# Two-layer hybrid decoder trunk: the RWKV blocks of the mixing projection move to 5th, 10th and 15th place, and a pair's preparation is placed after the tail two pairs back

## The chip, the cores and the metric

One core of one Trainium2 chip runs the whole program. The metric is the device time of one execution in microseconds (us). Runs of the kernel before are compared by their median; a profile is one further execution, recorded by the hardware profiler.

## The reference

The kernel computes two decoder layers over 256 tokens of width 2048, in float32. Each layer is a token-mixing part and a feed-forward part, each between two RMS norms:

```python
for l in range(DEPTH):                                   # DEPTH = 2
    u = rms_norm(h, norm_pre_mix[l])
    p = u @ w_in[l]
    p_ret, p_hgrn, p_ml, p_rw = split_cols(p, GROUP_COLS)
    o_ret  = retention_group(p_ret)
    o_hgrn = hgrn2_group(p_hgrn, ...)
    o_ml   = mlstm_group(p_ml, ...)
    o_rw, v_first = rwkv7_group(p_rw, v_first, ...)
    mixed = concatenate([o_ret, o_hgrn, o_ml, o_rw]) @ w_out[l]
    h = h + rms_norm(mixed, norm_post_mix[l])
    u = rms_norm(h, norm_pre_ffn[l])
    h = h + rms_norm((silu(u @ w_ffn_gate[l]) * (u @ w_ffn_up[l])) @ w_ffn_down[l], norm_post_ffn[l])
```

Each of the four groups has 8 heads of 64. The change concerns the RWKV-7 group, a recurrence over time with a full state matrix per head:

```python
state = state * exp(lw_t) - (state @ kk_t) (a_t * kk_t)^T + v_t k_t^T
y_t   = state @ r_t
```

## The kernel before

A matmul of float32 is made from three: each weight is split in a high and a low part, and so is the activation; hi·hi, hi·lo and lo·hi are summed. SyncE (SP) loads the weights in units (L239), ScalarE (ACT) makes `w_hi` (L247) and VectorE (DVE) `w_lo` (L248), TensorE (PE) multiplies (L300 is the helper of all matmuls, L304 of all transposes). GpSimd (POOL) does little.

The projection of the mixing stage is cut into 31 blocks of 256 columns. A block is 96 matmuls of 256 columns, called *main* matmuls here, and fills one of three accumulator banks in PSUM, `acc_85`, `acc_86` and `acc_87` (the name ends in a buffer number). The first three blocks are `lora`, `rwv0` and `rwv1`. The others follow the list `SEQ` (L78): an entry ("rw", j) is one block with the receptance and key columns of RWKV pair j (two heads), and an entry of another group (ml, hg, rt) is four blocks for half of that group's heads. So the RWKV blocks stand at places 4, 9, 14 and 19 of 31. The out projection follows with 288 wide matmuls of 512 columns and two narrow blocks.

Between the main matmuls stands the work on the heads, in many small steps that use all engines. A planner, `interleave`, writes the program: it counts TensorE's time in `self.pe` by an estimate, runs `stream` (the main matmuls) and, whenever the estimate says that a step of another process is due, places that step. `stream` is blocked when no bank is free, and then steps of the other processes follow each other with no main matmul between them. The engines then run their instructions in the order written, each waiting for semaphores. `settle` and `empty` drain a full bank: block rw_j goes with a token shift into `rk[j % 2]`, and not before pair j - 2 has read that buffer for the last time, which sets `rk_free`.

The work on RWKV pair j has three steps:

- `rw_head` (L1332), the preparation: decay, scan (`cpd`), the norm of the key over the head by matmuls `pr<-parts,blkr`, two reciprocals, and the operand `BK`. `head_proc` (L881) starts it after block rw_j is drained and `rw_mid` says that pair j - 1 is past its inner inverse.
- `rwkv` (L1379), the chain: the gram product `pr<-KVR,BK` into `G`; a 16-row triangular inverse on DVE (`sprod`, 15 steps), with its operands sent through DRAM on both sides (`LD`, L1410, and `XD`, L1449); the mask product `TDD`; then products that build the whole inverse, `pr<-TDD,LoT`, `pr<-TDD,rk` and `pr<-rk,TDD`, `pr<-kap,G` and `pr<-TT,kap`; then four sequential steps over the state `S`; then the output `pr<-S,KVR`. After `TT` is written (L1478), `rk` may be overwritten.
- `rw_tail` (L1531): layer norm over the head, the transpose `pr<-ident,kap`, the gate product `pr<-SG,gup`, and the result in `mx`. When both pairs of a half are done, `settle` splits `mx` into `m` for the out projection.

The buffers `rk`, `kap`, `ra` (a), `cpd`, `rwc` and `bonus` exist twice and are used by pair number modulo 2. Small products go to two further banks, `pr_88` and `pr_89`, in turn; `po_90` to `po_92` serve the other groups, and at the end of the stage the out projection too.

Of the kernel before, what the change touches and what calls it, by code (L numbers as in the profile page):

```python
# [34 lines left out]
NEVER = 1e9  # L35
# [39 lines left out]

BLOCK_COLS = _block_cols()
GATE = {"ml": "mlo", "hg": "hgg", "rt": "rtg"}
SEQ = [("rw", 0), ("hg", 0), ("rw", 1), ("ml", 0), ("rw", 2), ("hg", 1), ("rw", 3), ("rt", 0), ("ml", 1), ("rt", 1)]  # L78
BLOCKS = ["lora", "rwv0", "rwv1"]
for _m, _i in SEQ:  # L80
    BLOCKS += [f"rw{_i}"] if _m == "rw" else [f"{_m}v{_i}", f"{_m}{2 * _i}", f"{_m}{2 * _i + 1}", f"{GATE[_m]}{_i}"]
# [190 lines left out]
class Trunk:  # L272
# [451 lines left out]
    def interleave(self):  # L724


        self.t0 = self.pe
        self.order = [x for x in SEQ if x[0] != "rw"]
        self.free = list(self.S)
        self.full, self.got, self.gate_at, self.head_at, self.rw_mid, self.rk_free = [], {}, {}, {}, 0, 0  # L730
        self.grp_fin, self.v_fin, self.proj_fin = 0, self.l == 0, False
        self.left = {key: 2 for key in MIXED}
        self.mh, self.ml = [None] * 8, [None] * 8
        self.yws = []
        self.procs = [[self.pe, self.rw_proc()], [self.pe, self.grp_proc()]]
        stream = self.stream()
        while stream is not None or self.procs:
            self.settle()
            now = [p for p in self.procs if self.ready(p) <= self.pe]
            if now:  # L740
                p = now[0]
                r = next(p[1], "end")
                if r == "end":
                    self.procs.remove(p)
                else:
                    p[0] = r if callable(r) else self.pe + r
                continue
            r = next(stream, "end") if stream is not None else "blocked"
            if r == "end":
                stream = None  # L750
            elif r == "blocked" and not self.settle():
                t = min([self.ready(p) for p in self.procs])
                assert t < NEVER
                self.pe = max(self.pe, t)
# [126 lines left out]
    def head_proc(self):  # L881
        for j in range(4):
            yield self.after(f"rw{j}", LAT)
            yield lambda: self.pe if self.rw_mid >= j else NEVER
            yield from self.rw_head(j)
            self.head_at[j] = self.pe + HEAD

# [643 lines left out]
    def rw_tail(self, j, out):  # L1531

        nc = self.nc
        c4, r, k, kap, a, cpd, rc, t2 = self.rw_parts(j)
        yt, yc = kap.rearrange("p (t h e) -> p h t e", t=2, h=2), self.F[3]
        mean, var = rc[:, 0:4], rc[:, 4:8]
        nc.vector.tensor_reduce(out=mean.rearrange("p (h t) -> p h t", h=2), in_=yt, axis=mybir.AxisListType.X, op=ALU.add)
        self.ts(mean, mean, -1.0 / HD)
        hts = [(2 * hh + t, hh, t) for hh in range(2) for t in range(2)]
        for g, hh, t in hts:  # L1540
            self.act(yc[:, 64 * g:64 * g + 64], yt[:, hh, t, :], AF.Square, bias=mean[:, g:g + 1], accum_out=var[:, g:g + 1])
        self.ts(var, var, 1.0 / HD, LN_EPS)
        self.pw(rc[:, 8:12], var, -0.5)
        for g, hh, t in hts:
            self.ts(yt[:, hh, t, :], yt[:, hh, t, :], mean[:, g:g + 1], rc[:, 8 + g:9 + g], ALU.add, ALU.mult)
        yield 4.5 + RLAT
        ps = self.ret_bank()
        for t in range(2):
            self.tr(ps[:, 128 * t:128 * t + 128], kap[:, 128 * t:128 * t + 128])
        self.stt(yc, ps[:, 0:256], self.pcol("ln_w", j), t2)  # L1550
        ps = self.ret_bank()
        self.mm(ps[:, 0:256], self.gup[:, 128 * j:128 * j + 128], self.SG)
        self.mul(out, yc, ps[:, 0:256])
        self.left["rw", j // 2] -= 1

    def run(self):
        self.setup()
        self.plan()
        self.l = 0
        self.first_norm()  # L1560
        for l in range(self.layers):
            self.mixing()
            self.ffn()
# [19 lines left out]
```

## Time and profile before

| | us |
|---|---|
| median of 3 runs | 2670.57 (2667.83 to 2671.69) |
| profiled execution | 2666.12 |
| its span, first to last instruction | 2664.2 |
| TensorE busy | 2608.6 (98%) |
| VectorE busy | 1705.3 (64%) |
| ScalarE busy | 1297.5 (49%) |
| GpSimd busy | 63.9 (2%) |

The mean granted clock of TensorE over the span is 0.991. In layer 0 the mixing stage's heads lie between about 90 and 540 us, in layer 1 between about 1420 and 1865 us. A timeline row reads: start, duration, engine, line, operation, output <- inputs, shapes, count, and in brackets the idle time before it with what ended it. A row of the table of stretches gives busy times and, in parentheses, counts.

### The profile page before, as it was taken

The page shows a single profiled execution, that of the slowest core. Times are in us where ns is not written, and L with a number is a line of the kernel's source. Part 1 is how long each engine was busy: PE and PEld are TensorE (multiplying, and loading weights), DVE is VectorE, ACT ScalarE, POOL GpSimd, SP SyncE. Part 2 cuts the span into 40 slices and gives each one's busy share as a digit, 9 for nine tenths or more (in the row PEclk, how much of TensorE's full clock was granted, in tenths as well). Part 3 has the DMA queues.
Part 4 walks back from the last instruction along what each step waited for, and adds up shares of the span by engine and source line. Part 5 has one row for each costly group of instructions (what it writes and reads, how often), then busy time and mean ns, then how long its engine had stood idle before and what let it go on. Part 6 is the DMA issues. An engine that isn't in the chain of part 4 may idle for free.

```text
span 2664.2 us, 44425 instructions
## 1 busy us (share of the span) xinstructions
PE 2608.6 (98%) x17540; PEld 2344.9 (88%) x17540; DVE 1705.3 (64%) x3025; ACT 1297.5 (49%) x2129; POOL 63.9 (2%) x121
## 2 busy tenths in 40 slices
PE   8999999989999999999999999999999999999998
PEld 7999999778888888888999999997888888888888
DVE  6877878576555555445578788785755555554444
ACT  5454445456444444444464544454664444444442
POOL 0000000000000000000000000000000000000000
PEclk9999999989999999999999999999999999999999
DMA  7544455546666666666645444555466666666664
GB/s 234 168 139 135 131 156 150 172 129 189 189 189 188 187 188 189 192 199 196 192 151 161 144 131 140 148 154 150 147 193 189 187 188 188 189 189 192 198 201 143
DMA packets 149457, 459.30 MB, mean 172 GB/s; under 512 B 29120, under 2 KB 39936, under 8 KB 149248
## 3 DMA queue, kind: packets, MB, share of 16 engines
q1 hardware_dynamic: 148576, 455.81, 57.4%
q8 instruction: 137, 2.24, 0.3%
q10 hardware_dynamic: 672, 0.66, 0.1%
q14 instruction: 72, 0.59, 0.1%
HBM read 450.90 MB, written 3.41 MB: 171 GB/s over the span
## 4 chain that ended last, share of the span: by engine, by line
PE 96%; DVE 2%; DMA 1%; issue 0%; ACT 0%; POOL 0%; SPq 0%; POOLq 0%; DVEq 0%; ACTq 0%
PE acc L300 55%; PE po L300 28%; PE pr L300 12%; DVE w_lo L248 1%; PE pr L304 1%; PE po L304 0%; DVE h L292 0%; DVE un L288 0%; DMA h<-in_x 0%; DVE A L279 0%; DMA bp<-in_bpost 0%; DMA XD<-kap 0%; POOL small L310 0%; SPq L341 0%; ACT junk L295 0%
## 5 line engine op out<-in xcount | busy, mean ns | idle before, releaser
L248 DVE TENSOR_TENSOR w_lo<-w_raw,w_hi 128x1024 fp32r<-128x1024 f32 x840 | 1027.4, 1223 | 748.8 <-ACT w_hi L247 735.8
L247 ACT ACTIVATE w_hi<-w_raw 128x1024 fp32r<-128x1024 f32 x840 | 889.1, 1059 | 982.8 <-PE po L300 340.3
L300 PE MATMUL acc<-u,w_hi 128*128 128x256 f32 (+1 forms) x4256 | 999.8, 315 | 0.6 <-DVE u L292 0.5
L300 PE MATMUL acc<-u,w_lo 128*128 128x256 f32 x2656 | 750.5, 284 | 0.8 <-DVE w_lo L248 0.8
L300 PEld LDWEIGHTS acc<-u,w_hi 128*128 128x128 f32 x4256 | 701.6, 191 | 55.3 <-issue 5.1
L300 PEld LDWEIGHTS acc<-u,w_lo 128*128 128x128 f32 x2656 | 506.1, 191 | 6.5 <-DVE w_lo L248 1.0
L300 PE MATMUL po<-u,w_hi 128*128 128x512 f32 x1056 | 384.2, 396 | 0.0
L300 PE MATMUL po<-u,w_lo 128*128 128x256 f32 x1056 | 289.8, 279 | 0.0
L300 PE MATMUL pr<-u,w_hi 128*128 128x512 f32 x704 | 245.5, 396 | 0.0
L300 PEld LDWEIGHTS po<-u,w_hi 128*128 128x128 f32 x1056 | 196.6, 188 | 44.5
L300 PEld LDWEIGHTS po<-u,w_lo 128*128 128x128 f32 x1056 | 199.2, 189 | 3.7
L300 PE MATMUL pr<-u,w_lo 128*128 128x256 f32 x704 | 192.5, 279 | 0.0
L300 PE MATMUL acc<-w_hi,ah 128*128 128x256 f32 (+1 forms) x528 | 177.5, 336 | 0.0
L300 PE MATMUL acc<-w_lo,ah 128*128 128x256 f32 (+1 forms) x528 | 177.5, 336 | 0.0
L300 PE MATMUL acc<-w_hi,al 128*128 128x256 f32 (+1 forms) x528 | 177.4, 336 | 0.0
L300 PEld LDWEIGHTS pr<-u,w_hi 128*128 128x128 f32 x704 | 130.3, 188 | 29.4
L300 PE MATMUL acc<-w_hi,u 128*128 128x256 f32 (+1 forms) x768 | 148.6, 289 | 0.0
L300 PEld LDWEIGHTS pr<-u,w_lo 128*128 128x128 f32 x704 | 132.6, 188 | 2.1
L300 PE MATMUL po<-w_hi,al 128*128 128x512 f32 (+1 forms) x352 | 127.6, 363 | 0.0
L300 PE MATMUL po<-w_hi,ah 128*128 128x512 f32 (+1 forms) x352 | 127.6, 363 | 0.0
L300 PE MATMUL po<-w_lo,ah 128*128 128x512 f32 (+1 forms) x352 | 127.6, 363 | 0.0
L300 PEld LDWEIGHTS acc<-w_hi,u 128*128 128x128 f32 x768 | 120.7, 191 | 2.4 <-issue 1.2
(291 smaller groups left out, 2963.6 us busy)
## 6 DMA issues: line engine op xcount, KB each, us to landing
w_raw<-in_wgu SPq DMA_DIRECT2D x352, 512.0 KB, 4.5
w_raw<-in_win SPq DMA_DIRECT2D x240, 512.0 KB, 4.0
w_raw<-in_wdn SPq DMA_DIRECT2D x132, 512.0 KB, 3.7
w_raw<-in_wout SPq DMA_DIRECT2D x48, 512.0 KB, 3.7
w_raw<-in_wdnn SPq DMA_DIRECT2D x44, 512.0 KB, 3.6
w_raw<-in_woutn SPq DMA_DIRECT2D x16, 512.0 KB
w_raw<-in_wmv SPq DMA_DIRECT2D x8, 544.0 KB, 3.7
bp<-in_bpost SPq DMA_DIRECT2D x32, 128.0 KB, 3.5
```

The source lines that it names most:

```text
L247: self.nc.scalar.activation(hi, t, AF.Copy)
L248: self.nc.vector.tensor_tensor(out=lo, in0=t, in1=hi.bitcast(F32), op=ALU.subtract)
L300: self.nc.tensor.matmul(out, lhsT=lhsT, rhs=rhs, start=start, stop=stop, skip_group_check=True)
L304: self.nc.tensor.transpose(out, a, self.ident[0:n, 0:n])
```

## The change

Two entries of `SEQ` move, so that the RWKV blocks stand at places 4, 5, 10 and 15 of 31. And `head_proc` places the head of pair j only when the tail of pair j - 2 has been placed (`rw_done`), since both use the same half of `kap`, `ra`, `cpd`, `rwc` and `bonus`. This is a condition in the planner, not a wait on the chip.

```diff
-SEQ = [("rw", 0), ("hg", 0), ("rw", 1), ("ml", 0), ("rw", 2), ("hg", 1), ("rw", 3), ("rt", 0), ("ml", 1), ("rt", 1)]
+SEQ = [("rw", 0), ("rw", 1), ("hg", 0), ("rw", 2), ("ml", 0), ("rw", 3), ("hg", 1), ("rt", 0), ("ml", 1), ("rt", 1)]
...
-        self.full, self.got, self.gate_at, self.head_at, self.rw_mid, self.rk_free = [], {}, {}, {}, 0, 0
+        self.full, self.got, self.gate_at, self.head_at, self.rw_mid, self.rk_free, self.rw_done = [], {}, {}, {}, 0, 0, 0
...
-            yield lambda: self.pe if self.rw_mid >= j else NEVER
+
+            yield lambda: self.pe if self.rw_mid >= j and self.rw_done >= j - 1 else NEVER
...
         self.left["rw", j // 2] -= 1
+        self.rw_done = j + 1
```

How the program moves shows best at two places. The first is the middle of pair 1's chain in layer 0, on TensorE, from the last transpose of an mLSTM pair (`po<-ident,A`) to the product of `TDD` and `LoT`. `acc` rows are main matmuls, `u` the activations. Before:

```order
L304 MATMUL po_91<-ident,A_1_2_358 128x128 x2
L300 MATMUL acc_85<-u,w_lo 128x256
L300 MATMUL acc_86<-u,w_hi 128x256 x2
L300 MATMUL acc_86<-u,w_lo 128x256
...
L300 MATMUL pr_88<-TDD,LoT 64x64 x8
L300 MATMUL acc_86<-u,w_lo 128x256
```

After, from the mLSTM products (`po<-mlv,P`) to the first main matmuls of the 17th block:

```order
L300 MATMUL po_91<-mlv,P_350 128x65 x6
L300 MATMUL po_92<-mlv,P_351 128x65 x6
L304 MATMUL po_90<-ident,A_1_0_356 128x128 x2
L300 MATMUL pr_89<-TDD,LoT 64x64 x8
L304 MATMUL po_91<-ident,A_1_2_358 128x128 x2
L300 MATMUL pr_89<-TDD,rk_320 64x64 x8
L300 MATMUL pr_88<-parts,blkr 128x256 x4
L300 MATMUL pr_88<-rk_320,TDD 32x32 x8
L300 MATMUL pr_88<-kap_316,G 32x32 x8
L300 MATMUL pr_89<-TT,kap_316 32x32
L300 MATMUL acc_86<-u,w_hi 128x256 x2
L300 MATMUL acc_86<-u,w_lo 128x256
```

The main matmuls between the steps are gone, the head of pair 2 (`parts`) stands inside the chain of pair 1, and the next main matmul writes `acc_86`, the bank of pair 3's block.

On DVE the same place, from the products that need `TDD` to the copy of `kap` ahead of TT. Before:

```order
L248 TENSOR_TENSOR w_lo<-w_raw,w_hi 128x1024
L279 TENSOR_TENSOR kap_316<-TDD,pr_89 32x4x32 x2
L279 TENSOR_TENSOR TT<-TDD,pr_88 64x4x64 x2
L248 TENSOR_TENSOR w_lo<-w_raw,w_hi 128x1024
L1482 COPY kap_316<-pr_89 32x4x32
```

After; the two rows that read `acc_86` drain pair 3's block:

```order
L292 SCALAR_TENSOR_TENSOR F_314<-rk_319,prm 128x256
L279 TENSOR_TENSOR parts<-F_314,parts 128x256
L287 TENSOR_SCALAR F_313<-pr_88 128x256
L279 TENSOR_TENSOR bonus_338<-v_308,pr_88 128x256
L1372 RECIPROCAL F_313<-F_313 128x256
L279 TENSOR_TENSOR kap_316<-TDD,pr_88 32x4x32 x2
L292 SCALAR_TENSOR_TENSOR rk_320<-acc_86,omu,shp_304 128x256
L279 TENSOR_TENSOR ra_317<-ra_317,F_313 128x256
L1377 RECIPROCAL F_313<-cpd_334 128x256
L292 SCALAR_TENSOR_TENSOR rk_320<-acc_86,omu,shp_304 128x256
L1483 COPY kap_316<-pr_88 32x4x32
```

Weight splits (`w_lo`) have left this stretch, and pair 2's head with its two reciprocals has come into it.

The second place is the end of RWKV's work in layer 0, on TensorE; `acc` and `po` rows with `m` are wide matmuls of the out projection. Before:

```order
L300 MATMUL po_91<-w_lo,m 128x512
L300 MATMUL pr_89<-S_332,KD 128x64
L300 MATMUL pr_88<-F_312,TT 128x64
L300 MATMUL pr_89<-KVT,G 64x64 x4
L300 MATMUL pr_89<-S_332,KVR 64x64 x3
L300 MATMUL pr_88<-KVT,G 64x64 x4
L300 MATMUL pr_88<-S_332,KVR 64x64 x3
L300 MATMUL pr_88<-SG,gup 128x256
L304 MATMUL pr_89<-ident,kap_316 128x128 x2
L300 MATMUL acc_86<-w_hi,m 128x512
```

After, around the same last transpose:

```order
L300 MATMUL acc_86<-w_lo,m 128x512
L300 MATMUL acc_87<-w_hi,m 128x512 x2
L304 MATMUL pr_89<-ident,kap_316 128x128 x2
L300 MATMUL acc_87<-w_lo,m 128x512
L300 MATMUL acc_85<-w_hi,m 128x512 x2
```

Before, nothing but the last pair stands there. After, wide matmuls stand on both sides: 47 from the last `S,KVR` to the transpose, and 25 from there to the last 72, which need this pair. In layer 1, 12 stand between `S,KVR` and the transpose, and none behind it.

## The prediction

> **What bounds the kernel now.** I read the page's totals first.
>
> ```profile
> span 2664.2 us, 44425 instructions
> PE 2608.6 (98%) x17540; PEld 2344.9 (88%) x17540; DVE 1705.3 (64%) x3025; ACT 1297.5 (49%) x2129; POOL 63.9 (2%) x121
> PEclk9999999989999999999999999999999999999999
> ```
>
> TensorE is busy for 2608.6 of 2664.2 us, so an order of work can win only the 55.6 us in which it idles, and loses whatever idle time it adds. Next the table of stretches, for the mixing stages of both layers. Its columns are the length, the busy time of PE, PEld, DVE, ACT and POOL with their counts, the granted clock, the DMA share and GB/s.
>
> ```profile
> core 0: us, PE busy (x) PEld busy (x) DVE busy (x) ACT busy (x) POOL busy (x), PEclk, DMA share, GB/s
> 240.00:350.00 110.00, 110.00 (x990) 105.06 (x988) 90.94 (x217) 49.47 (x83) 4.95 (x7) 1.00 0.49 146
> 470.00:556.00 86.00, 78.82 (x407) 63.97 (x406) 44.79 (x77) 35.33 (x62) 3.95 (x5) 0.94 0.51 148
> 1570.00:1680.00 110.00, 110.00 (x983) 104.10 (x981) 92.95 (x223) 48.64 (x85) 4.58 (x7) 1.00 0.48 142
> 1800.00:1880.00 80.00, 73.42 (x370) 58.90 (x370) 41.09 (x68) 33.11 (x54) 3.51 (x5) 0.94 0.49 146
> ```
>
> While the blocks are projected TensorE has no idle time at all; DVE is at 83% there (90.94 of 110). Only the ends idle, by 7.2 us (86.00 - 78.82) and 6.6 us (80.00 - 73.42). The timeline of TensorE and the table for those two places:
>
> ```profile
> 530.15 0.44 PE L300 MATMUL pr<-S,KVR 64*64 64x64 f32 x6
> 535.44 0.66 PE L304 MATMUL pr<-ident,kap 128*128 128x128 f32 x2 [3.77 <-DVE kap L288]
> 538.32 1.65 PE L300 MATMUL acc<-w_hi,m 128*128 128x512 f32 x3 [2.21 <-ACT m L295]
> 527.18:538.32 11.14, 3.96 (x38) 2.56 (x36) 5.16 (x14) 4.10 (x13) 1.04 (x1) 0.73 0.31 96
> 538.32:542.63 4.31, 4.31 (x10) 3.48 (x11) 0.75 (x2) 0.00 (x0) 0.00 (x0) 0.50 0.00 0
> 1855.94 0.44 PE L300 MATMUL pr<-S,KVR 64*64 64x64 f32 x6
> 1861.22 0.66 PE L304 MATMUL pr<-ident,kap 128*128 128x128 f32 x2 [3.24 <-DVE kap L288]
> 1864.10 1.65 PE L300 MATMUL acc<-w_hi,m 128*128 128x512 f32 x3 [2.21 <-ACT m L295]
> 1852.96:1864.10 11.14, 4.56 (x37) 2.83 (x36) 5.15 (x14) 4.10 (x13) 1.04 (x1) 0.67 0.32 95
> 1864.10:1867.00 2.90, 2.90 (x7) 2.32 (x8) 0.75 (x2) 0.00 (x0) 0.00 (x0) 0.50 0.03 6
> ```
>
> The last RWKV pair closes alone: its output product S,KVR, its tail (the transpose ident,kap waits 3.77 us for DVE), then `m` from ACT, for which the out projection's last 72 wide matmuls wait. TensorE restarts at half clock, 0.50 for 4.31 us in layer 0 and 2.90 in layer 1, which costs half of that time again: 2.15 and 1.45 us.
>
> What matters for the new order is how long one pair's chain is, from its gram product (pr<-KVR,BK) to its last triangular product (pr<-TT,kap), and what stands beside it. First and last row of pair 1 in both layers, then the stretches of pair 1 and pair 0 (layer 0, then 1):
>
> ```profile
> 205.38 1.71 PE L300 MATMUL pr<-KVR,BK 64*128 64x128 f32 x16
> 256.08 0.24 PE L300 MATMUL pr<-TT,kap 32*32 32x32 f32 x2
> 1534.40 0.82 PE L300 MATMUL pr<-KVR,BK 64*128 64x128 f32 x7
> 1586.48 0.24 PE L300 MATMUL pr<-TT,kap 32*32 32x32 f32 x2
> 205.38:256.08 50.70, 50.70 (x460) 48.17 (x459) 37.93 (x103) 26.48 (x48) 3.46 (x4) 1.00 0.47 134
> 1534.40:1586.48 52.08, 52.08 (x474) 49.69 (x474) 41.40 (x113) 27.75 (x52) 3.31 (x4) 1.00 0.49 141
> 92.94:148.08 55.14, 54.86 (x515) 53.65 (x514) 46.16 (x125) 21.23 (x29) 0.00 (x0) 1.00 0.51 149
> 1421.80:1481.63 59.83, 59.83 (x557) 58.16 (x557) 49.46 (x138) 25.30 (x39) 2.52 (x4) 1.00 0.49 141
> ```
>
> The chain takes 51 to 60 us, and TensorE notices nothing because some 300 main matmuls stand beside it in its program. One main matmul of 256 columns is 0.12 us (228 in 27.34), a wide one of 512 columns 0.226 us (14 in 3.17), from the chain of waits:
>
> ```profile
> 26.71 27.34 PE acc L300 x228
> 501.81 3.17 PE acc L300 x14
> ```
>
> Two thirds and more of the chain is work in DVE's queue (37.93 of 50.70 us, 41.40 of 52.08), and part of the rest is two trips of data through DRAM that no engine can speed up:
>
> ```profile
> 212.24 0.60 SPq L1410 DMA_DIRECT2D LD<-F  x1
> 219.99 0.16 DVE L279 TENSOR_TENSOR sprod<-F,F 32x15 f32<-32x15 f32 x1 [2.25 <-DMA F<-LD]
> 237.67 0.33 SPq L1449 DMA_DIRECT2D XD<-F  x1
> 243.27 0.69 DVE L279 TENSOR_TENSOR TDD<-F,cst 128x512 f32<-128x512 f32 x1 [2.18 <-DMA F<-XD]
> ```
>
> They are 7.75 us (212.24 to 219.99) and 5.60 us (237.67 to 243.27).
>
> **The change, part by part.** Amounts of work do not change: the matmuls, the weight loads on SP and the splits on ACT and DVE are the same in number and size, POOL's queue is untouched, and SP only takes the same blocks in another order. All terms are therefore idle time on TensorE.
>
> *The added wait.* It is no semaphore but a condition for where the head of pair j goes in the program. It binds for pair 2 alone, whose head stands at most 30 main matmuls later, 3.6 us; pair 0 and 1 meet it at once, and pair 3's head is held by other conditions. Behind it on TensorE stand main matmuls that do not need it, so its own price is 0; at most 3.6 us of it lengthens pair 2's chain, which has 391 mains beside it (313 before) and lies nowhere on the end's path.
>
> *The 16th block, layer 0.* Pair 3's projection is now the 15th block, and its bank can be drained only into the `rk` buffer that pair 1 still reads. Three banks are filled, so after 16 blocks (1536 mains) TensorE's program holds no main until pair 1's chain is through: LoT, rk, the head of pair 2, G and TT,kap follow each other with nothing between. Gram to that point now has 125 mains instead of 300; the small matmuls in it hardly change (96 for 90). So 175 x 0.12 = 21.0 us of cover are gone. Half of DVE's weight splits leave the chain (12 to 6), but the head of pair 2 enters it, of which these rows give the large part:
>
> ```profile
> L248 DVE TENSOR_TENSOR w_lo<-w_raw,w_hi 128x1024 fp32r<-128x1024 f32 x840 | 1027.4, 1223 | 748.8 <-ACT w_hi L247 735.8
> L1376 DVE RECIPROCAL F<-cpd 128x256 f32<-128x256 f32 x8 | 14.0, 1745 | 0.0
> L1371 DVE RECIPROCAL F<-F 128x256 f32<-128x256 f32 x8 | 14.0, 1745 | 0.0
> L292 DVE SCALAR_TENSOR_TENSOR F<-F,F 128x256 f32<-128x256 f32 x40 | 16.9, 422 | 0.6
> L1347 DVE TENSOR_TENSOR_SCAN cpd<-F,zero 128x64 f32<-128x64 f32 x32 | 6.6, 268 | 0.0
> L279 DVE TENSOR_TENSOR parts<-F,parts 128x256 fp32r<-128x256 f32 x16 | 6.6, 415 | 0.0
> ```
>
> Out: 6 x 1.223 = 7.3 us. In: 2 x 1.745 + 5 x 0.422 + 4 x 0.268 + 2 x 0.415 = 7.5 us, and the two draining operations behind them. I add 1 us for these: **22 us**. Bounds: if all waits of the chain but DVE's work and its two DMA waits (2.25 and 2.18) vanish because TensorE answers at once, the chain is 42.4 us, 8.3 shorter: 14 us. If it is as long as the longest shown, 59.83, it is 9.1 longer: 31 us. I stay near the middle, since head and chain now share DVE at the tightest place.
>
> *The 16th block, layer 1.* The same with 153 mains for 311: 158 x 0.12 = 19.0, and 2 for DVE's queue (41.40 us busy here against 37.93), **21 us**. Bounds: 41.40 plus the same 4.4 is 45.8, 6.3 shorter: 15 us; with 59.83, 7.8 longer: 29 us.
>
> *Restart after both gaps.* Both are longer than the 11.14 us stretch that ended at 0.50 above, so I take its 2.15 us twice: **4.3 us** (0 to 4.3).
> The Trainium skill ("TensorE: Matmul & The Clock Gate", Part 1, "What's actually happening") says that the array falls to half rate after an idle window of about 3.4 us and returns after a busy one. By that figure a restart costs an estimated 1.7 us, and the sum would be 0.9 us lower. The trace agrees in kind, with 4.31 us at 0.50.
>
> *The 11th block.* Pair 0's chain now runs beside pair 1's head. In layer 1 a clump without mains stands before the 12th block (rk, G and TT,kap of pair 0), and in layer 0 mains stand between them. By durations DVE's queue there grows by 21.0 us in layer 0 and 19.3 in layer 1, while the mains beside the chain grow by 451 - 345 = 106 (12.7 us) and 427 - 360 = 67 (8.0 us). If DVE were the whole chain that would be 8 and 11 us; if its idle time (55.14 - 46.16 = 9.0 and 59.83 - 49.46 = 10.4) takes the surplus, 0. I take **2 and 5 us**, more for layer 1 because of the clump.
>
> *The end of layer 0.* The last S,KVR stands 72 wide matmuls before the out projection's last 72, where nothing stood behind it; the transpose stands 25 before them. 47 x 0.226 = 10.6 us cover the 5.29 from S,KVR to the transpose (530.15 to 535.44), and 25 x 0.226 = 5.7 us the 2.88 from there to the restart. The idle time (11.14 - 3.96 = 7.2) goes, with 2.15 of half clock and a little of the small matmuls' own latency: **10 us gained** (0 if the chain arrives late all the same; 11.1 + 2.15 at most).
>
> *The end of layer 1.* Here S,KVR has 12 wide matmuls behind it, 2.7 us, and the transpose none. 5.28 - 2.7 = 2.6 us of the wait stay, the 2.88 to the restart stays, and the half clock most likely too: **3 us gained** of the 6.6 idle (0 to 8.0, with the half clock).
>
> Sum: 22 + 21 + 4.3 + 2 + 5 - 10 - 3 = +41.3 us. The profiled execution took 2666.12 us (span 2664.2), 4.5 below the median of the runs, 2670.57. On the profiled execution that makes 2707.4, on the median **2712 us**.
>
> **The rivals.**
> *Faster: the chain shrinks into its cover.* In the trace each small matmul of the chain stands in line behind mains. With none ahead of it the chain might run much faster. The price: for each us that pair 1's chain loses, both gaps lose one. At 22 us less both are gone with their half clock, and if the 11th blocks are hidden too, only the ends remain, 2670.6 - 13 = 2657.6. It decides from about 20 us less, a chain of about 31 us (2 x 20 = 40 of the 41.3). Against it: DVE alone is busy for 37.93 us in it, and the two DMA trips take 13.3 us.
> The Trainium skill (same page, Part 2, "Step-by-step: what each phase is for") says that matmuls stay in program order and only weight loads are pulled ahead. By that, TensorE cannot fetch later mains into the gap, which speaks against this rival; no row here shows an attempt.
>
> *No change.* The same mechanism at 18 to 22 us less: about 2670. The same evidence speaks against it.
>
> *Much slower: the head is paid in full.* Pair 2's head, 7.5 us on DVE, stands in series with the chain, whose other waits do not shrink. At the high ends 31 + 29 + 4.3 + 8 + 11 - 13 = +70, 2741 us. For it: 83% of DVE's time is taken in these stretches. Against it: 7.3 us of splits leave the chain.
>
> *The change does nothing.* The order of the blocks is data that the program is built from; the rows of TensorE differ from the first RWKV block on, so I give this no chance of its own beyond "no change".
>
> **How the numbers follow.** The forecast gets 0.85, much slower 0.08, faster 0.04, no change 0.03. 0.2%, or 5.3 us, is about what a measurement can tell from no change; the forecast and the slow rival lie far above it, so slower has 0.93. For the range: both gaps at the low end (14 + 15) and the rest as taken give 2698; both at the high end (31 + 29) give 2729. With the other bounds (half clock 0, the 11th blocks at 0, or 8 and 11; gains at their ends) a few us lie outside on either side, so the range is 2692 to 2736, which leaves out most of the two fast rivals and half of the slow one.
>
> **What would show it.** In the changed trace TensorE should have a stretch of some 20 us with almost no main matmul, in each layer, at the 16th block, ended by a wait of acc for DVE's `rk` (the drained bank) and followed by a PEclk of 0.50. The row ident,kap in layer 0 should no longer wait 3.77 us with mains absent, and the 7.2 us at the end of layer 0 should be gone. Layer 1's end should still show an idle of about 5 us. The forecast is wrong if gram to TT,kap of pair 1 comes out under 40 us, if mains run between LoT and TT,kap, or if another wait, such as weights that arrive late after the gap, appears behind the restart.

## The result and the profile after

The changed kernel took 2704.98 us (median of 4 runs, 2703.84 to 2706.09), the kernel before 2669.2 in the same series: 1.0133 times as long, 95% interval 1.0115 to 1.0151, 35.8 us slower. Forecast were 2712 (2692 to 2736) and +41.3. The page's totals of after:

```profile
span 2701.9 us, 44408 instructions
PE 2620.1 (97%) x17540; PEld 2352.8 (87%) x17540; DVE 1711.4 (63%) x3025; ACT 1294.8 (48%) x2128; POOL 66.5 (2%) x121
PEclk9998999999999999999999989999899999999999
```

TensorE and VectorE do the same number of instructions. TensorE idles 81.8 us of the span (2701.9 - 2620.1) for 55.6 before, and is busy 11.5 us longer; in the rows below, the half clock stands where that shows. The clock line has 40 slices of 67.5 us: the 4th and the 24th (203 to 270 and 1554 to 1621 us) are below full speed now, and the 9th, where the end of layer 0's mixing stood before, is not; the 29th holds layer 1's end. The new standstill in layer 0, on TensorE's timeline:

```profile
250.78 1.12 PE L300 MATMUL pr<-TDD,LoT 64*64 64x64 f32 x16 [2.35 <-DVE TDD L279]
255.79 0.58 PE L300 MATMUL pr<-parts,blkr 128*128 128x256 f32 x1 [2.22 <-ACT parts L295]
260.87 0.64 PE L300 MATMUL pr<-rk,TDD 32*32 32x32 f32 x16 [0.84 <-DVE bonus L279]
262.96 0.64 PE L300 MATMUL pr<-kap,G 32*32 32x32 f32 x16 [1.46 <-DVE kap L279]
264.27 0.31 PE L300 MATMUL pr<-TT,kap 32*32 32x32 f32 x2 [0.68 <-ACT kap L295]
265.90 0.80 PE L300 MATMUL acc<-u,w_hi 128*128 128x256 f32 x2 [1.31 <-DVE rk L292]
```

Each small product waits for DVE or ACT, pair 2's head (`parts`) included, and the main matmuls come back only when DVE has drained pair 3's block into `rk`. The table of stretches has both standstills, the restart after the first, the clump of layer 1's 11th block, and the ends of both layers:

```profile
core 0: us, PE busy (x) PEld busy (x) DVE busy (x) ACT busy (x) POOL busy (x), PEclk, DMA share, GB/s
241.00:265.90 24.90, 12.41 (x103) 9.55 (x103) 20.55 (x65) 5.41 (x15) 2.07 (x2) 0.55 0.11 27
265.90:270.60 4.70, 4.70 (x33) 4.41 (x33) 1.78 (x5) 0.00 (x0) 0.42 (x2) 0.50 0.00 0
1583.00:1609.20 26.20, 9.25 (x93) 6.64 (x92) 19.26 (x59) 6.79 (x18) 2.02 (x2) 0.60 0.11 25
1497.00:1512.00 15.00, 11.79 (x130) 10.13 (x130) 13.83 (x36) 8.41 (x18) 3.06 (x6) 1.00 0.31 104
527.50:553.50 26.00, 26.00 (x136) 21.05 (x135) 14.75 (x22) 11.61 (x21) 1.04 (x1) 1.00 0.57 173
1886.00:1900.50 14.50, 9.14 (x57) 6.81 (x55) 7.06 (x15) 5.93 (x14) 1.04 (x1) 0.94 0.48 145
```

The end of layer 0 no longer idles at all; the end of layer 1 still does, by 5.4 us. How late the same matmul with split weights starts, after less before, read off both timelines (those of the out projection and the feed-forward part are counted too, from the start of the program):

| matmul | place | after less before, us |
|---|---|---|
| 1410 | ahead of layer 0's 16th block | -4.7 |
| 1560 | behind it | +24.0 |
| 3191 | ahead of the out projection's last part | +24.3 |
| 3500 | behind it | +10.8 |
| 8632 | ahead of layer 1's 11th block's end | +8.7 |
| 8652 | behind it | +16.2 |
| 9092 | ahead of layer 1's 16th block's end | +15.2 |
| 9152 | behind it | +43.1 |
| 10772 | ahead of the out projection's last part | +41.2 |
| 10992 | behind it | +37.4 |

So far this is the forecast. What the experiments ask is what makes the loss.

### The profile page after: what moved, and what is told of

Read it like the earlier page. It is cut to its first block, busy times and chain, and to the rows that moved or that the text cites. A ratio compares the mean times of both kernels' runs of the same rounds, so it can differ in the third digit from the quotient of the medians.

```text
span 2701.9 us, 44408 instructions
## 1 busy us (share of the span) xinstructions
PE 2620.1 (97%) x17540; PEld 2352.8 (87%) x17540; DVE 1711.4 (63%) x3025; ACT 1294.8 (48%) x2128; POOL 66.5 (2%) x121
## 4 chain that ended last, share of the span: by engine, by line
PE 95%; DVE 3%; ACT 1%; DMA 1%; issue 1%; SPq 0%; POOL 0%; ACTq 0%; POOLq 0%; DVEq 0%
PE acc L300 55%; PE po L300 27%; PE pr L300 12%; PE pr L304 1%; PE po L304 0%; DVE h L292 0%; DVE w_lo L248 0%; DVE un L288 0%; DMA h<-in_x 0%; ACT junk L295 0%; ACT w_hi L247 0%; DMA XD<-kap 0%; DVE F L292 0%; DMA F<-XD 0%; DVE P L292 0%
## 5 line engine op out<-in xcount | busy, mean ns | idle before, releaser
L248 DVE TENSOR_TENSOR w_lo<-w_raw,w_hi 128x1024 fp32r<-128x1024 f32 (+1 forms) x840 | 1028.0, 1224 | 774.8 <-ACT w_hi L247 768.6
L247 ACT ACTIVATE w_hi<-w_raw 128x1024 fp32r<-128x1024 f32 (+1 forms) x840 | 888.8, 1059 | 990.7 <-PE po L300 338.3
```

Source lines behind the costliest of these rows:

```text
L247: self.nc.scalar.activation(hi, t, AF.Copy)
L248: self.nc.vector.tensor_tensor(out=lo, in0=t, in1=hi.bitcast(F32), op=ALU.subtract)
```

## The experiments

Two theories. **A**, by which the sum was made: the loss is the standstill itself, and it comes from a bank that cannot be drained. **B**: the four pairs' chains follow each other and are about as long as the whole stage, so that the loss is whatever makes the chains longer; where the standstill shows is secondary. In the old order of blocks the added condition alone changes no engine's program, so that was not run.

**Another bank.** In the changed kernel the 17th block takes the bank of pair 3 only because, in the planner, it asks ahead of the draining of the 16th. The edit lets the planner drain first, and puts pair 3's bank last in the list of free ones.

```diff
             self.full.append((n, accs))
+            yield
...
+            self.free.sort(key=lambda b: b is self.last_rw)
             accs, self.free = self.free[:n], self.free[n:]
...
                 self.free += accs
+                if n == "rw3":
+                    self.last_rw = accs[0]
```

> The changed kernel, with the 17th block sent into one of the two banks that the 16th leaves, not into the one that holds pair 3's projection; nothing else is edited. Theory A (the loss is the stall at the 16th block, about 25 us in layer 0 and 27 in layer 1, made by that bank; the rest of the change is sound): the stall goes, the gain at the ends stays, 2653 us (2645 to 2665). Theory B (the four pairs follow each other in one chain that is about as long as the stage, and an early head only lengthens each pair's part; while TensorE stood still the chain got ahead of the main matmuls): no stall at the 16th block, but pair 1 and 2 take about 113 us each again, the chain of layer 0 ends near 560 us, and TensorE stands still at the end of the projection and of the out projection instead: 2700 to 2730 us, not faster than the changed kernel by more than 5 us.

2706.63 us, 1.0145 (1.013 to 1.016). The table of stretches of this run, pair 1 from gram to TT, the place of the old standstill, then the two new ones of layer 0:

```profile
213.28:284.05 70.77, 70.77 (x630) 67.54 (x629) 59.57 (x147) 34.81 (x58) 3.31 (x4) 1.00 0.45 137
235.00:270.00 35.00, 35.00 (x310) 34.00 (x310) 28.75 (x75) 18.77 (x32) 2.01 (x2) 1.00 0.44 133
443.00:454.50 11.50, 6.34 (x57) 5.36 (x57) 5.59 (x16) 3.60 (x13) 1.04 (x1) 0.65 0.29 91
537.00:556.00 19.00, 10.36 (x56) 7.31 (x55) 8.45 (x22) 4.80 (x15) 1.48 (x2) 0.63 0.27 83
```

The standstill at the 16th block is gone without a trace, and not one us is won: pair 1's chain takes 70.8 us for the 47.8 it had while TensorE stood still, and TensorE waits for the pairs at 443 and at 537 instead. Theory A was 54 us off; B has this run in its range. The same stretch of pair 1's chain in after, and then the weight splits (L248) in it, in after and in this run:

```profile
216.48:264.27 47.79, 35.57 (x292) 30.70 (x291) 38.40 (x115) 19.15 (x38) 3.37 (x4) 0.78 0.28 82
216.48:264.27 47.79, 7.35 (x7) 0.78 0.28 82
213.28:284.05 70.77, 21.98 (x19) 1.00 0.45 137
```

VectorE works 59.6 us in the chain at full pace, 22.0 of it splits for the main matmuls; while TensorE stands still it does 7.35 us of them. The standstill bought a faster chain. The chain is 23.0 us longer at full pace, and VectorE is busy 21.2 us longer in it (59.57 - 38.40): 14.6 of that are splits, 6.5 other work. Its idle time in the chain grows by 1.8 us only, so little is left for small products that wait behind main matmuls.

**Three rk buffers** take the hold on the bank away at the other side: pair 3's block can be drained before pair 1 has read its own.

```diff
-        self.rk = [t([128, 2, 256], f"rk{i}") for i in range(2)]
+        self.rk = [t([128, 2, 256], f"rk{i}") for i in range(3)]
...
-            if self.rk_free < d - 1:
+            if self.rk_free < d - 2:
... (rk[d % 3] and rk[j % 3] where rk[d % 2] and rk[q] stood)
```

> The changed kernel with three rk buffers, so that pair 3's block can be drained before pair 1 has read its own: the cause of the 16th block's stall is taken away in another way than by the bank. Theory A: 2653 us (2645 to 2665). Theory B: the same as with the other bank, pairs 1 and 2 near 70 us from gram to TT, and idle time at the ends of both layers: 2702 us (2690 to 2715).

2700.48 us, 1.0123 (1.0107 to 1.0138), as B has it; A's 2653 is out. Pair 1 and 2 take 67.4 and 65.9 us, TensorE has no idle time in pair 1's chain, and the ends idle by 8.7 and 9.2 us. Pair 1, then the ends:

```profile
213.19:280.62 67.43, 67.43 (x594) 63.96 (x593) 56.43 (x140) 33.26 (x57) 4.25 (x4) 1.00 0.45 137
534.00:551.00 17.00, 8.28 (x50) 5.72 (x49) 7.35 (x20) 4.35 (x14) 1.04 (x1) 0.69 0.26 81
1879.00:1897.00 18.00, 8.83 (x51) 6.29 (x50) 7.85 (x20) 4.24 (x14) 1.04 (x1) 0.68 0.26 80
```

**The head behind the chain.**

```diff
-            yield lambda: self.pe if self.rw_mid >= j and self.rw_done >= j - 1 else NEVER
+            yield lambda: self.pe if self.rw_mid >= j and self.rw_done >= j - 1 and self.rk_free >= j else NEVER
```

> The changed kernel, but the head of pair j is placed only when pair j-1 has written its inverse TT, so no head stands inside a chain; the order of the blocks is the changed one. Pair 1's gram product then stands 253 (layer 0) and 175 (layer 1) main matmuls before the end of the 16th block, for 125 and 153. Theory A (only the bank's stall counts): the stall shrinks by 128 x 0.12 = 15 us in layer 0 and 22 x 0.12 = 3 us in layer 1, 2687 us (2680 to 2692). Theory B (heads inside the chain lengthen the chain): beside that, pair 1's gram to TT falls under 45 us, because 7.5 us of head work leave it, pair 0's chain falls from 69.7 to about 55 us, and layer 1's end is covered too: 2660 us (2650 to 2672), faster than the kernel before.

2667.5 us, 0.9996 (0.9987 to 1.0005): the whole loss is gone with one condition, and the order of blocks is still the changed one. Theory A's 2687 is out; of B's range it is the upper part, and B's "faster than the kernel before" did not come true. Pairs 0 and 1 of layer 0, the splits in each, the two places at the 16th block (layer 0, layer 1), and both ends:

```profile
94.12:143.81 49.69, 48.79 (x453) 46.57 (x452) 40.39 (x103) 19.17 (x29) 0.00 (x0) 1.00 0.48 145
202.44:251.81 49.37, 45.74 (x419) 42.60 (x418) 37.65 (x103) 25.59 (x46) 3.31 (x4) 0.98 0.44 133
94.12:143.81 49.69, 15.80 (x13) 1.00 0.48 145
202.44:251.81 49.37, 14.41 (x12) 0.98 0.44 133
240.00:253.00 13.00, 9.37 (x114) 7.97 (x113) 9.28 (x20) 6.02 (x10) 0.00 (x0) 0.88 0.43 132
1565.00:1578.00 13.00, 5.11 (x65) 4.08 (x65) 7.00 (x28) 2.81 (x9) 2.01 (x2) 0.72 0.20 50
515.00:535.00 20.00, 20.00 (x91) 16.50 (x90) 11.75 (x16) 9.34 (x11) 1.01 (x1) 1.00 0.57 167
1850.00:1870.00 20.00, 20.00 (x90) 16.50 (x89) 11.70 (x18) 9.74 (x17) 1.04 (x1) 1.00 0.55 165
```

The same pair 0 in after, with the head of pair 1 in its chain, and the splits in it:

```profile
94.00:163.70 69.70, 69.70 (x629) 67.68 (x628) 62.11 (x151) 28.89 (x43) 0.00 (x0) 1.00 0.49 147
94.00:163.70 69.70, 23.33 (x19) 1.00 0.49 147
```

Pair 0's chain, 69.7 us in after, is 49.7; both ends are covered now, and about 3.6 and 7.9 us of idle time stay at the 16th blocks. Pair 1's chain came out at 49.4, not under 45 as expected: with more main matmuls beside it, it also has 12 splits instead of 7.

**Pair 1's block early, pairs 2 and 3 where they were.**

```diff
-SEQ = [("rw", 0), ("rw", 1), ("hg", 0), ("rw", 2), ("ml", 0), ("rw", 3), ("hg", 1), ("rt", 0), ("ml", 1), ("rt", 1)]
+SEQ = [("rw", 0), ("rw", 1), ("hg", 0), ("ml", 0), ("rw", 2), ("hg", 1), ("rw", 3), ("rt", 0), ("ml", 1), ("rt", 1)]
```

> The changed kernel with the RWKV blocks in places 4, 5, 14 and 19: pair 1's block early, pair 2 and 3 where they were. No bank is held across pair 1's chain. Theory A: no stall anywhere but at the ends, which are as before: 2669 us (2664 to 2675). Theory B: head 1 stands inside pair 0's chain (459 main matmuls from gram to TT for 345), the pairs end later, and the ends idle longer, by about one state step in layer 0 (4 us) and two in layer 1 (8 us): 2681 us (2675 to 2688).

2681.7 us, 1.005 (1.0035 to 1.0065), as B has it. No bank is held, and there is no standstill in the middle; pair 0's chain with head 1 in it, and the ends:

```profile
93.86:164.50 70.64, 70.64 (x637) 68.65 (x636) 61.97 (x153) 32.21 (x47) 0.00 (x0) 1.00 0.49 148
527.00:545.80 18.80, 10.08 (x55) 7.18 (x54) 7.62 (x20) 5.03 (x15) 1.22 (x2) 0.63 0.28 84
1861.00:1880.00 19.00, 9.72 (x54) 6.76 (x53) 8.25 (x22) 4.35 (x14) 2.43 (x2) 0.65 0.24 77
```

One early head costs 13.6 us by itself. It shows at the ends, where 8.7 and 9.3 us are idle, for 7.2 and 6.6 before, and where the granted clock is 0.63 and 0.65: across them the delay after the kernel before grows by 5.0 us in layer 0 (matmul 3180 to 3200 of the count above) and by 12.2 in layer 1 (10600 to 10800).

**Pair 1's block back, pairs 2 and 3 early** (`rw0, hg0, rw1, rw2, ml0, rw3, hg1, rt0, ml1, rt1`).

> The changed kernel with the RWKV blocks in places 4, 9, 10 and 15: only pair 1's block goes back. The 11th block's clump in layer 1 is gone (7.5 us), and pair 1's gram in layer 0 stands 238 main matmuls before the stall for 125; layer 1 keeps 153. Theory A: 2705 - 7.5 - 113 x 0.12 = 2684 us (2677 to 2690). Theory B: the same price for layer 1's stall, and pair 0's chain back at 55 and 60 us, so the end of layer 0 comes about 10 us earlier than in the changed kernel, which the main matmuls cover already: 2684 us too (2677 to 2692). What it tells apart is the share of pair 1's early block (about 20 us) from that of pair 3's (the rest).

2694.32 us, 1.0102 (1.0085 to 1.0118): 10 us above both expectations and outside both ranges. This is 26.2 us above the kernel before, so pair 1's early block makes the other 9.6 of the 35.8 us of the change; alone it cost 13.6, so the shares do not add up exactly. What I had wrong is layer 0: pair 1's chain still has head 2 in it, and took 56.7 us instead of the 47.8 that I had carried over:

```profile
203.21:259.92 56.71, 47.24 (x408) 42.72 (x407) 46.73 (x126) 26.88 (x51) 4.45 (x4) 0.92 0.38 116
```

**Without the condition** (the new list on the kernel before). This kernel leaves out what keeps pair 2's head behind pair 0's tail on the buffers that both use, so it does not compute pair 0 as the reference does; it stands here for its time alone.

> The kernel before with the new list alone, without the added condition; pair 2's head may then be placed ahead of pair 0's tail, which works on the same buffers, so the numbers of pair 0 need not be the reference's. It prices the condition in the new order. Both theories: head 2 stands in pair 1's chain with or without it, the 16th block is the same, and pair 0's tail only comes later: 2705 us (2700 to 2709). A rival, that the condition itself makes the loss by holding pair 2's head back: under 2690 us.

2713.1 us, 1.0166 (1.0149 to 1.0183), 8 us slower than with it and outside the expected range; the two intervals just touch (1.0115 to 1.0151 with it). In this order the condition does not cost time but seems to save some: without it pair 0's tail goes into the standstill too (its transpose in layer 0 stands at 246.99 us, for 226.19), and pair 1's chain is 53.5 and 56.2 us for 47.8 and 53.8.

```profile
215.63:269.17 53.54, 37.03 (x288) 32.59 (x287) 37.50 (x106) 19.05 (x38) 2.30 (x3) 0.70 0.26 73
1560.37:1616.56 56.19, 40.39 (x316) 35.95 (x315) 39.34 (x107) 20.93 (x41) 2.30 (x3) 0.73 0.28 79
```

**The late head and the other bank together.**

> Both edits together: the late head and the 17th block in a free bank. It asks whether the stall that the late head still has at the 16th block (3.5 and 7.9 us idle) can simply be taken away. Theory A (a stall is a loss by itself): 2667.5 - 11.3 idle - 4.3 of half clock = 2652 us (2648 to 2658). Theory B (chain and main matmuls are in balance, and a chain that shares VectorE with splits at full pace ends later): no stall at the 16th block, pair 1 from gram to TT 53 us or more, and idle time at the ends again, 5 to 7 us in layer 0 and 8 to 10 in layer 1: 2670 us (2664 to 2677).

2674.35 us, 1.002 (1.0011 to 1.0029). Even the small standstill of the late head can't be taken away for nothing: pair 1 goes from 49.4 to 57.3 us, and the ends idle by 7.3 and 8.7 us (its median is 6.9 us above that of the late head alone):

```profile
201.72:259.00 57.28, 57.28 (x509) 53.74 (x508) 42.87 (x109) 29.65 (x52) 3.27 (x4) 1.00 0.44 133
530.00:542.20 12.20, 4.90 (x36) 3.23 (x35) 5.52 (x15) 3.81 (x12) 1.04 (x1) 0.74 0.36 109
1855.00:1873.00 18.00, 9.35 (x53) 6.53 (x52) 8.16 (x22) 4.35 (x14) 1.48 (x2) 0.65 0.27 82
```

**The late head and the changed order in layer 0, the order of before in layer 1.**

```diff
-        for n in BLOCKS[3:]:
+        for n in BY_LAYER[self.l][3:]:
```

> The late head with the changed order of blocks in layer 0 alone; layer 1 has the order of before. In the late head's trace layer 0 was 3.5 us ahead of the kernel before after its out projection and layer 1 gave 4.3 us back. If the layers are independent (both theories): 2668.1 - 3.5 = 2664.6 us (2661.5 to 2667.5), 0.13% faster than before, at the edge of what can be measured.

2664.62 us (11 runs), 0.9985 (0.9976 to 0.9994): the one version that beats both, the kernel before by 4 us; the interval excludes "no change", though not by much.

The runs in one view. "Chain" is the time from pair 0's gram product to pair 3's transpose, read off TensorE's timelines; its change is that of both layers' sum, the time's change that of the median against the kernel before in the same series.

| kernel | chain layer 0 | chain layer 1 | chain's change | time's change |
|---|---|---|---|---|
| before | 442.5 | 439.4 | | |
| without the condition | 458.1 | 467.3 | +43.5 | +45 |
| other bank | 458.6 | 460.5 | +37.2 | +38 |
| after | 451.5 | 462.8 | +32.4 | +36 |
| three rk | 453.9 | 458.0 | +30.0 | +32 |
| pair 1 back | 446.5 | 460.4 | +25.0 | +26 |
| pair 1 early only | 448.8 | 448.2 | +15.1 | +14 |
| late head, other bank | 444.9 | 444.1 | +7.1 | +6 |
| late head | 428.9 | 440.4 | -12.6 | -1 |
| late head in layer 0 | 428.6 | 439.6 | -13.7 | -4 |

Wherever the chains are longer than before, the time follows them within 4 us, whether TensorE stands still at the 16th block, at the ends or at both. Where they are shorter, little of it is won: the main matmuls and the remaining standstill set the time then.

## Why the prediction was right, and where its reason was not

*The sum.* 41.3 us were forecast and 35.8 measured (37.7 between the two profiled executions' spans). The three terms of layer 0 ahead of its end (22, half of 4.3, 2) make 26.2; the table shows 24.3 - 0.7 = 23.6, the 0.7 being a later start of the first main matmul. Its end gained 13.5 (24.3 to 10.8) for the 10 forecast, just beyond the upper bound. In layer 1 the 11th block cost 7.5 for 5, the 16th 27.9 for 21 + 2.15, the end gave 3.8 for 3.

*The size of the standstill.* Pair 1's chain to TT took 47.8 us in layer 0 and 53.8 in layer 1. I had 50.7 and 52.1 and 1 or 2 us for the head's work, right within 4 us. That is because two things nearly cancel, as the prediction had it: the splits that leave (12 before, 7 after) and the head that comes. VectorE is busy 38.40 us in the chain, for 37.93 before.

*The step that failed* is "175 x 0.12 = 21.0 us of cover are gone", read as a cause. The amount was right, since a standing TensorE is a standing TensorE. But the text made it a matter of the bank: "Three banks are filled". That held for a moment only. The 16th block is one of values, which takes two banks, and ScalarE had emptied both by 238.9 us:

```profile
237.26 0.38 ACT L295 ACTIVATE vt<-acc 128x256 f32<-128x256 f32 x1 [0.57 <-PE acc L300]
238.52 0.37 ACT L295 ACTIVATE vt<-acc 128x256 f32<-128x256 f32 x1
```

Giving the 17th block one of these two changed the time by 1.7 us. Nor did the planner stand blocked there. It can drain pair 3's block only after it has placed pair 1's `TT`, and it gave the 17th block that bank, drained, before it drained the 16th; yet ScalarE drains the 16th at 237 us and does `rk<-pr`, a step of pair 1 that `TT` needs, only at 251.95. So the engines do not run in the planner's order alone: the kernel leaves the final order to a scheduler (`schedule_with_timeline_sim=True`).

What the runs put in place of the bank: head j + 1 has come into chain j, whose length, from `KVR,BK` to `TT,kap`, goes from 48 to 60 us without a head (all eight pairs of before) to 66 to 76 with one at full pace (pairs 0 and 2 of after, pairs 0 to 2 with the other bank and with three rk, pair 0 with pair 1's block early). The four chains in series, 442.5 us in layer 0 before, are about as long as the stage, which lies between 90 and 540 us; so TensorE must wait for them somewhere. With the head moved behind TT, everything else as changed, the loss was 0.

*The 11th block*, costed at 2 and 5 us, belongs to the same mechanism. Pair 0's chain grew by 14.6 us in layer 0 (55.1 to 69.7); I looked only at whether TensorE would stand still there, and it did not. The delay was passed on to pair 1, and came due at the 16th block as the 125 main matmuls that I counted.

*The added wait* was costed at 0, at most 3.6 us. In the new order it seems to save about 8, by keeping pair 0's tail out of pair 1's chain.

*The half clock* held: 0.50 for the 4.70 us after layer 0's restart, 2.35 us lost for the 2.15 taken; in layer 1 it is 0.69 over the 5 us from 1609 to 1614, 1.6 us lost.

*The rivals.* Pair 1's chain did not run in 31 us, as the fast rival needed: it took 47.8, and the shortest chain of all runs is 43.2 (pair 3 of layer 1 with three rk). The much slower rival put the head in series with an unshortened chain; the run with the other bank comes nearest to that, and it is only 1.7 us slower than after, since with no standstill the delay falls due at the ends.

The 20.0 us between pair 0's chain with and without a head (69.70 and 49.69) go with VectorE's work in it: 62.11 and 40.39 us, 21.7 more. 7.5 of these are further splits (23.33 and 15.80). The other 14.2 are the head, counted at 7.5 in the prediction from a part of its rows, and steps of the other groups; these two are not separated. In every chain whose row stands in this document, the length less VectorE's busy time is 7.6 to 16.9 us, while the length goes from 47.8 to 70.8. That VectorE's queue sets the chain's length is read from this; no run takes the splits or the head's work off VectorE to test it.

## What to carry to other kernels

When a chain of small steps runs beside a stream of large matmuls, price a change first by what it puts into the chain's own queues, and only then by what TensorE does beside it. A standstill shows where a delay falls due, and here it was not the cause: before taking a blocked buffer for the culprit, give it another buffer and see whether the idle time only moves. Work that becomes possible earlier is not free to do earlier, if it shares an engine with the chain that bounds the stage.

## What the runs showed of the hardware

The granted clock does not go by the amount of idle time alone. It stayed at 1.00 in the 15 us of the 11th block's clump, although TensorE idled for 3.2 us in it, 1.71 of them in one piece. In the late head's layer 1, 13 us with 7.9 us of idle time were granted 0.72. And at the beginning of after's standstill in layer 0 it fell while TensorE was busy most of the time:

```profile
235.00:240.00 5.00, 4.50 (x31) 3.87 (x30) 4.93 (x17) 4.08 (x7) 0.00 (x0) 1.00 0.43 137
240.00:245.00 5.00, 4.19 (x27) 3.79 (x25) 4.63 (x19) 1.09 (x4) 0.00 (x0) 0.83 0.36 105
245.00:250.00 5.00, 2.11 (x9) 1.52 (x8) 2.67 (x15) 0.73 (x3) 2.07 (x2) 0.50 0.16 26
239.54 0.92 PE L300 MATMUL po<-A 64*128 64x256 f32 x4 [0.50 <-DVE P L292]
241.28 0.92 PE L300 MATMUL po<-A 64*128 64x256 f32 x4 [0.81 <-DVE P L292]
242.12 4.30 PE L300 MATMUL po<-mlv,P 128*128 128x65 f32 x24
247.75 0.69 PE L304 MATMUL po<-ident,A 128*128 128x128 f32 x2 [1.33 <-DVE A L279]
```

The clock is 0.83 on average from 240 to 245 us and 0.50 from 245 on, so it fell before 245. Up to there the longest idle piece in these rows is 0.81 us, and from 242.12 on TensorE ran 24 narrow products without a break. So no long idle piece is needed for the clock to fall; what it does go by, these rows do not show.
